# Expert weights w1 and w3 read in 8 KB runs, with token rows transposed by every fourth column

## The chip, the cores and the metric

The kernel runs on one core of a Trainium2 chip, as one program of 34,524 instructions. The metric is the device time of an execution in microseconds; of the kernel before there are three timed runs and one profiled execution. A core has five engines that run side by side: TensorE (PE in the profile, with its weight loads shown apart as PEld), VectorE (DVE), ScalarE (ACT), GpSimd (POOL) and SyncE (SP). SP computes nothing here; it issues most of the transfers between the main memory (DRAM) and the on-chip memory, which 16 DMA engines carry out.

## The reference

One encoder block over 1024 tokens of 1024 channels, in float32. Its first half mixes tokens; its second half, which the change touches, is a mixture of experts:

```
g_logits = xt @ w_rg + b_rg                       # one group of 8
_, g_sel = top_k(g_logits, 1)
e_logits = (xt @ w_re + b_re)[group g_sel]        # 8 experts of that group
top_v, top_i = top_k(e_logits, 2)
weights = softmax(g_logits)[g_sel] * softmax(top_v)
...
hdn = silu(xb @ w1[e]) * (xb @ w3[e])             # w1[e], w3[e]: 1024 x 512
ys  = hdn @ w2[e]                                 # w2[e]: 512 x 1024
out[token] += weight * ys
...
x = layer_norm(ALPHA * x + out)
```

There are 64 experts, each with 6 MB of weights, so the weights of all of them are 403 MB, and each is read once. A matrix product sums over the rows of w1 and w3; in which order it sums does not matter, as long as the tokens' channels are taken in the same order.

## The kernel before, in words

The first half (input projection, convolution, gated linear attention, gates, output projection, first layer norm and router) ends at about 1000 us. It leaves the tokens' rows both in on-chip memory (`x1`) and in a DRAM scratch (`x1_d`).

The expert half works on tiles of 128 rows. Ranked by how many tokens they have, the experts get 128, 64 or 32 rows of a tile, and a fixed string, PATTERN, gives the order of the 29 tiles: an "o" tile is one expert with 128 rows, a "d" tile two with 64, a "q" tile four with 32. For a tile GpSimd clears `xgp` (L1364) and gathers 128 token rows into it with an indirect DMA (`gather`, L1196). `make_xt` (L1204) then transposes `xgp` on TensorE, in 8 blocks of 128 columns, and ScalarE copies the result to `xT` (L1205): 128 partitions, 8 blocks k, 128 tokens. In `make_xt` the operand that the PE loads as weights is the block of `xgp`; what streams past it is the identity matrix.

`job_h` (L1420) multiplies one expert's rows: for k from 0 to 7 it takes block k of `xT` and, of w1 and then of w3, the 512 values that each partition holds for block k. After the activation, `job_t` (L1434) transposes the result, and `job_y` (L1452, L1455) multiplies it with w2. `combine` (L1507) adds finished tiles to the tokens' rows by products with 0/1 matrices, woven in between the steps of later jobs.

The weights come through one queue. `w_pieces` cuts an expert into six pieces of 1 MB: w1, w3 and w2 in two halves each. `load_piece` (L941) issues one piece into one slot of 128 partitions x 8 KB; a half of w1 or w3 is 512 rows of 512 values, a half of w2 is 256 rows of 1024 values. The pieces are issued by SP, in the order in which the tiles need them. `pump_w` issues the next piece only when a slot has been given free, and jobs give slots free as they finish with a piece (`release`). About 16 to 19 slots are in use for weights, some three experts ahead. 382 of the 384 pieces are issued by SP, two by GpSimd.

The lines that fix how rows of w1 and w3 lie on the partitions are the DMA's access pattern, here with r = 512 and f = 512,

```
eng.dma_start(out=t.rearrange("p (k f) -> p k f", f=f),
              in_=m.rearrange("o r f -> (o r) f")[i * r:(i + 1) * r].rearrange("(k p) f -> p k f", p=128))
```

by which partition p holds rows p, 128 + p, 256 + p and 384 + p of the half, four runs of 2 KB, and the blocks that `make_xt` transposes, columns (4h + k) x 128 to (4h + k + 1) x 128, whose column p lands on partition p.

Of the kernel before, what the change touches and what calls it, by code (L numbers as in the profile page):

```python
# [54 lines left out]
assert (1 + N64) % 2 == 0 and N32 % 4 == 0  # L55
OVB = NT * 128
RND = float(3 << 22)


def _order():  # L60
# [22 lines left out]
def tile_block(ctx: ExitStack, tc: tile.TileContext, x, w_in, b_in, conv_w, conv_b, conv_ln_g,  # L83
# [5 lines left out]
    out = out[0]  # L89
# [13 lines left out]
    def slot(dt, name):  # L103
        return SP.tile([128, 2048], dt, tag="slot", name=name, bufs=NS)
# [13 lines left out]
    TE = nc.tensor  # L118
# [13 lines left out]
    ident = CP.tile([128, 128], F32, name="ident")  # L132
# [117 lines left out]
    def load_x(i):  # L250
        t = slot(F32, f"x{i}")
        for c in (slice(0, 512), slice(512, DM)) if i < 2 else (slice(0, DM),):
# [9 lines left out]
                      in_=w_in[:, C_F:C_F + 16].rearrange("(k p) c -> p k c", p=128))  # L262
# [606 lines left out]
    def mmb(shape=(128, 512), name="psb"):  # L869
        return PB.tile(list(shape), F32, tag="mm", name=name, bufs=5)  # L870
# [60 lines left out]
    def load_piece(wt, pc, t=None, eng=nc.sync):  # L931
        nm, src, i, e = pc
        if t is None:
            t = slot(F32, f"{nm}_{i}")
        if isinstance(e, int):
            m = src[e:e + 1]
        else:
            m = src[bass.ds(e(), 1)]
        r = 512 if nm != "w2" else 256
        f = 512 if nm != "w2" else 1024  # L940
        eng.dma_start(out=t.rearrange("p (k f) -> p k f", f=f),  # L941
                          in_=m.rearrange("o r f -> (o r) f")[i * r:(i + 1) * r].rearrange("(k p) f -> p k f", p=128))
        wt.setdefault(nm, []).append(t)

    rank_reg = {}
# [25 lines left out]
    def pump_w(eng=nc.sync):  # L971
        while queue and free[0] > 0 and (queue[0][0][0] == "s" or known):
            key, pc = queue.popleft()
            load_piece(wts_of[key], pc, eng=eng)
            free[0] -= 1
# [128 lines left out]
    xgp = CB.tile([128, DM], F32, name="xgp")  # L1104
# [95 lines left out]
    def make_xt(xT):  # L1200
        for h in range(2):
            ps = mmb((128, 4, 128), "psxT")
            for k in range(4):
                TE.transpose(ps[:, k, :], xgp[:, (4 * h + k) * 128:(4 * h + k + 1) * 128], ident)  # L1204
            A.copy(xT[:, 4 * h:4 * h + 4, :], ps)  # L1205

    static_map(0)
# [42 lines left out]
    V.tensor_scalar(c1[:, 0:16], i128[E64], ov, None, op0=OP.is_lt)  # L1250
    V.tensor_reduce(nb, c1[:, 0:16], axis=AX.X, op=OP.add)
    make_xt(rtm[:, 1024:2048].rearrange("p (k t) -> p k t", k=8))
    gather(tix[:, 1:2])
    prw = smb((128, 512), "psrow")
# [37 lines left out]
    rows = rt1[:, 832:1024].rearrange("p (a e) -> p a e", e=64)  # L1292
# [27 lines left out]
    V.tensor_scalar(hi, s16, -63.5, 1.0 / 128.0, op0=OP.add, op1=OP.mult)  # L1320
    V.tensor_scalar(hi, hi, RND, None, op0=OP.add)
    V.tensor_scalar(hi, hi, RND, None, op0=OP.subtract)
    V.scalar_tensor_tensor(lo, hi, -128.0, s16, op0=OP.mult, op1=OP.add)
# [47 lines left out]
    def turn_rows(s):  # L1371
        s["xT"] = WB.tile([128, 8, 128], F32, name="xTp", bufs=2)
        make_xt(s["xT"])
# [242 lines left out]
    class OnUse(dict):  # L1616
# [5 lines left out]
        def __missing__(self, nm):  # L1622
            for pc in w_pieces(self.e):
                if pc[0] == nm:
                    load_piece(self, pc, self.tiles[pc[2]])
            return self[nm]
# [140 lines left out]
```

## Time and profile before

| | us |
|---|---|
| median of three runs | 2072.95 |
| the three runs | 2072.12 to 2077.11 |
| the profiled execution | 2076.78 |
| its span | 2075.0 |

| engine | busy us | share of the span |
|---|---|---|
| PE | 1952.7 | 94% |
| PEld | 1432.0 | 69% |
| DVE | 1023.6 | 49% |
| ACT | 507.6 | 24% |
| POOL | 124.6 | 6% |

The span runs from the first to the last instruction; the execution's time has a little around it. A busy PE is not a PE at its peak: matmuls overlap, and the profile models their ends. The share of 94% is a mean over two halves that are limited in different ways, so the expert half has to be read by stretches. The DMA share is the mean of the 16 engines; it can pass 1 since an engine can have two packets under way at once. [...]

### The profile page before, as it was taken

How to read it: one execution, taken by the hardware profiler on the slowest of the kernel's cores; microseconds unless marked ns; L12 is line 12 of the kernel's file. 1: busy time of each engine (PE TensorE's matmuls, PEld its weight loads, DVE VectorE, ACT ScalarE, POOL GpSimd, SP SyncE). 2: the span in 40 equal slices, each digit the busy share in tenths (PEclk: the TensorE clock that was granted, in tenths of full speed). 3: DMA queues.
4: the chain of work that ended last, by engine and by line, in shares of the span. 5: the costliest groups of instructions: out<-in, count | busy, mean ns of one | idle time of the engine just before them, and what ended most of it. 6: DMA issues, size and time to landing. Idle time of an engine off the chain costs nothing.

```text
span 2075.0 us, 34524 instructions
## 1 busy us (share of the span) xinstructions
PE 1952.7 (94%) x14631; PEld 1432.0 (69%) x14631; DVE 1023.6 (49%) x1483; ACT 507.6 (24%) x959; POOL 124.6 (6%) x130
## 2 busy tenths in 40 slices
PE   8999999999999999999898997999979997999686
PEld 6898889888888778899645565555655565555453
DVE  4777777878886475566631332223312332223156
ACT  5323342232222343211212121111121121121112
POOL 0000000000000130000100000000000000000000
PEclk9999999999999999999899998999999998999898
DMA  5101210243333536256799999999999999999995
GB/s 168 46 21 44 102 66 21 67 144 138 122 122 142 223 106 204 102 197 240 273 368 394 352 393 394 394 394 393 356 393 393 393 393 394 393 392 393 392 394 210
DMA packets 236749, 525.43 MB, mean 253 GB/s; under 512 B 11730, under 2 KB 53802, under 8 KB 236592
## 3 DMA queue, kind: packets, MB, share of 16 engines
q1 hardware_dynamic: 223808, 482.91, 63.0%
q0 software_dynamic: 12784, 40.28, 5.2%
q8 instruction: 116, 1.90, 0.4%
q14 instruction: 41, 0.34, 0.0%
HBM read 496.33 MB, written 34.08 MB: 256 GB/s over the span
## 4 chain that ended last, share of the span: by engine, by line
PE 37%; DMA 9%; DVE 2%; ACT 1%; issue 1%; SPq 1%; POOLq 0%; ACTq 0%
PE psh L1420 16%; PE pscb L1507 9%; DMA w<-in_w_dram 9%; PE psy L1455 6%; PE psy L1452 2%; PE psxT L1204 1%; PE psacc L1544 1%; PE pshT L1434 1%; DVE x L1512 1%; SPq L941 0%; ACT yv L1465 0%; ACT yhl L1484 0%; DVE yhl L1485 0%; PE psbc L1685 0%; DVE rtm L1337 0%
## 5 line engine op out<-in xcount | busy, mean ns | idle before, releaser
L1420 PE MATMUL psh<-w,xTp 128*32 128x128 f32 (+2 forms) x5792 | 442.0, 326 | 68.0 <-DMA w<-in_w_dram 61.6
L1420 PEld LDWEIGHTS psh<-w,xTp 128*32 128x32 f32 (+2 forms) x5792 | 269.9, 124 | 222.0 <-issue 107.6
L586 DVE SCALAR_TENSOR_TENSOR c<-sg,cw,c 128x994 f32<-128x994 f32 (+14 forms) x240 | 310.0, 1292 | 5.4
L1512 DVE TENSOR_TENSOR x<-x,pscb 128x512 f32<-128x512 f32 x240 | 164.2, 687 | 231.1 <-PE pscb L1507 230.5
L1507 PE MATMUL pscb<-yhl,pt 128*128 128x512 f32 x896 | 268.5, 443 | 8.6 <-DVE pt L1500 6.8
L1507 PEld LDWEIGHTS pscb<-yhl,pt 128*128 128x128 f32 x896 | 162.4, 197 | 93.8 <-issue 33.0
L1455 PE MATMUL psy<-w,hT 128*32 128x256 f32 (+1 forms) x1408 | 150.6, 445 | 0.8 <-ACT hT L1436 0.8
L1427 DVE TENSOR_TENSOR hs<-hs,psh 128x128 f32<-128x128 f32 (+2 forms) x65 | 25.4, 391 | 235.6 <-ACT hs L1426 210.3
L1465 ACT COPY yv<-psy 32x256 f32<-32x256 f32 (+1 forms) x174 | 73.7, 423 | 213.2 <-PE psy L1455 211.3
L1436 ACT COPY hT<-pshT 128x128 f32<-128x128 f32 (+2 forms) x65 | 22.8, 350 | 365.6 <-PE pshT L1434 365.6
L1455 PEld LDWEIGHTS psy<-w,hT 128*32 128x32 f32 (+1 forms) x1408 | 56.6, 118 | 71.8 <-issue 51.7
L1485 DVE SCALAR_TENSOR_TENSOR yhl<-yv,tw,yhl 128x1024 fp32r<-128x1024 f32 x19 | 24.4, 1284 | 160.0 <-ACT yhl L1484 150.9
L1364 POOL MEMSET xgp<- 128x1024 f32 x27 | 25.7, 953 | 828.4 <-PE psxT L1204 828.4
L1452 PE MATMUL psy<-w,hT 128*128 128x512 f32 x144 | 64.0, 597 | 0.0
L1485 DVE SCALAR_TENSOR_TENSOR yhl<-psy,tw,yhl 128x512 fp32r<-128x512 f32 x18 | 13.5, 750 | 88.6 <-ACT yhl L1484 87.6
L1205 ACT COPY xTp<-psxT 128x512 f32<-128x512 f32 x56 | 30.1, 590 | 109.4 <-PE psxT L1204 108.9
L1452 PEld LDWEIGHTS psy<-w,hT 128*128 128x128 f32 x144 | 26.8, 190 | 32.5 <-issue 31.2
L1500 DVE TENSOR_TENSOR pt<-iof,ttok 128x256 fp32r<-128x256 f32 (+1 forms) x120 | 47.8, 400 | 0.0
L1426 ACT ACTIVATE hs<-psh 128x128 f32<-128x128 f32 (+2 forms) x65 | 23.5, 361 | 56.8 <-PE psh L1420 56.3
L1204 PEld LDWEIGHTS psxT<-ident,xgp 128*128 128x128 f32 x232 | 27.4, 143 | 9.1 <-issue 4.1
L1204 PE MATMUL psxT<-ident,xgp 128*128 128x128 f32 x232 | 31.1, 278 | 2.4 <-DVEq L1634 1.6
L502 DVE SCALAR_TENSOR_TENSOR st<-st,dec,pskv 128x256 f32<-128x256 f32 x60 | 28.8, 480 | 7.2 <-PE pskv L218 4.0
(653 smaller groups left out, 3849.1 us busy)
## 6 DMA issues: line engine op xcount, KB each, us to landing
w<-in_w_dram SPq DMA_DIRECT2D x382, 1024.0 KB, 14.0
x<-in_x_dram SPq DMA_DIRECT2D x6, 1024.0 KB, 8.2
o_d<-oT POOLq DMA_DIRECT2D x4, 1024.0 KB, 4.4
conv_d<-c POOLq DMA_DIRECT2D x4, 1024.0 KB, 4.7
or<-o_d SPq DMA_DIRECT2D x4, 1024.0 KB, 4.7
og_d<-or POOLq DMA_DIRECT2D x4, 1024.0 KB, 5.2
gb_d<-gb POOLq DMA_DIRECT2D x4, 1024.0 KB, 7.4
o<-og_d SPq DMA_DIRECT2D x4, 1024.0 KB, 5.8
```

The source lines that it names most:

```text
L502: V.scalar_tensor_tensor(o, prev, gla["dec", p][:, hh, c:c + 1], pk[b][:, a, :], op0=OP.mult, op1=OP.add)
L586: V.scalar_tensor_tensor(c[:, s:], u[:, :SEQ - s], w, c[:, s:], op0=OP.mult, op1=OP.add)
L1204: TE.transpose(ps[:, k, :], xgp[:, (4 * h + k) * 128:(4 * h + k + 1) * 128], ident)
L1205: A.copy(xT[:, 4 * h:4 * h + 4, :], ps)
L1420: TE.matmul(p_[j * cap:(j + 1) * cap, :], s["xT"][:, k, so:so + cap], w_[k // 4][:, (k % 4) * 512 + j * n:(k % 4) * 512 + (j + 1) * n], st ...
L1452: TE.matmul(pys[h], lh, w_[:, h * 512:(h + 1) * 512], start=(f == 0), stop=(f == 3))
L1455: TE.matmul(pys[0][j * cap:(j + 1) * cap, 0:n], lh, w_[:, j * n:(j + 1) * n], start=(f == 0), stop=(f == 3), skip_group_check=True)
L1465: (V.tensor_copy if j % 2 and "same" in s and q["last"] else A.copy)(s["y"][so:so + cap, j * n:(j + 1) * n], pys[0][j * cap:(j + 1) * cap, ...
L1485: V.scalar_tensor_tensor(s["hl"][:, 1024 + c:1024 + c + n], y, s["w"], f32(hi), op0=OP.mult, op1=OP.subtract)
L1500: V.tensor_tensor(pts[tt][:, 0:n, :], iof[:, None, :].to_broadcast([128, n, 128]), tk[:, :, None].to_broadcast([128, n, 128]), op=OP.is_equal)
L1507: TE.matmul(ps, pts[tt][:, a, :], s["hl"][:, i * 1024 + h * 512:i * 1024 + (h + 1) * 512], start=(a + i == 0), stop=(a == n - 1 and i == 1))
L1512: V.tensor_tensor(xa, xa, ps, op=OP.add)
```

## The change

Half a matrix of w1 or w3 (512 rows) is laid on the partitions with four neighbouring rows on each: partition p holds rows 4p to 4p + 3, one run of 8 KB in DRAM. Block k of a partition is then row 4p + k. So that the products still match, `make_xt` transposes, for half h and block k, the columns h x 512 + k, h x 512 + k + 4, and so on: every fourth column of `xgp`, 128 of them. w2 is loaded as before, and so is everything else. The two places use the same lists of pieces and the same tiles; on every engine the instructions and their order are the same, and only the shape of 256 transfers and the step of 232 transposes' reads differ.

```diff
+RUNS = ("w1", "w3")
...
         r = 512 if nm != "w2" else 256
         f = 512 if nm != "w2" else 1024
-        eng.dma_start(out=t.rearrange("p (k f) -> p k f", f=f),
-                          in_=m.rearrange("o r f -> (o r) f")[i * r:(i + 1) * r].rearrange("(k p) f -> p k f", p=128))
+        rows = m.rearrange("o r f -> (o r) f")[i * r:(i + 1) * r]
+        if nm in RUNS:
+
+            eng.dma_start(out=t, in_=rows.rearrange("(p k) f -> p (k f)", p=128))
+        else:
+            eng.dma_start(out=t.rearrange("p (k f) -> p k f", f=f), in_=rows.rearrange("(k p) f -> p k f", p=128))
         wt.setdefault(nm, []).append(t)
...
             for k in range(4):
-                TE.transpose(ps[:, k, :], xgp[:, (4 * h + k) * 128:(4 * h + k + 1) * 128], ident)
+                TE.transpose(ps[:, k, :], xgp[:, h * 512 + k:(h + 1) * 512:4], ident)
             A.copy(xT[:, 4 * h:4 * h + 4, :], ps)
```

## Rows read from the trace of the kernel before

**Rows 1.** Line L941, SP: instructions, duration ns min/median/max, first and last start us.

```profile
L941 SPq DMA_DIRECT2D w<-in_w_dram x382: 367/2198/6328, 921.7 to 2030.6; - x191
```

**Rows 2.** Busy time by stretches, from 1078 us on.

```profile
core 0: us, PE busy (x) PEld busy (x) DVE busy (x) ACT busy (x) POOL busy (x), PEclk, DMA share, GB/s
1078.00:1118.00 40.00, 31.77 (x653) 21.88 (x653) 8.12 (x15) 10.63 (x27) 3.88 (x4) 0.99 1.04 394
1118.00:1166.00 48.00, 46.22 (x189) 25.83 (x189) 15.65 (x26) 5.58 (x11) 1.95 (x2) 0.94 1.02 385
...
1190.00:1305.00 115.00, 97.68 (x1300) 66.26 (x1293) 31.09 (x57) 21.95 (x55) 5.85 (x6) 0.94 1.04 394
1305.00:1418.00 113.00, 111.67 (x580) 62.07 (x581) 29.12 (x48) 20.29 (x37) 7.79 (x8) 0.99 1.04 394
1418.00:1500.00 82.00, 82.00 (x507) 48.71 (x509) 26.71 (x47) 11.39 (x20) 3.90 (x4) 1.00 0.99 369
1500.00:1541.00 41.00, 29.71 (x578) 20.74 (x572) 4.63 (x9) 10.75 (x29) 1.95 (x2) 0.95 1.04 393
1541.00:1640.00 99.00, 99.00 (x484) 57.17 (x484) 30.92 (x53) 14.13 (x26) 7.80 (x8) 0.99 1.04 393
1640.00:1771.00 131.00, 117.87 (x1490) 77.01 (x1487) 33.26 (x60) 26.07 (x61) 5.85 (x6) 0.95 1.04 393
1771.00:1982.00 211.00, 191.37 (x1596) 116.44 (x1599) 53.22 (x92) 38.07 (x77) 10.83 (x12) 0.96 1.04 393
1982.00:2034.00 52.00, 47.80 (x406) 24.19 (x406) 31.86 (x55) 7.58 (x17) 0.00 (x0) 0.93 1.04 392
```

**Rows 3.** The same view in steps of 5 us, around the queue's pauses.

```profile
1165.00:1170.00 5.00, 5.00 (x38) 2.79 (x38) 1.50 (x2) 1.38 (x2) 0.00 (x0) 1.00 0.24 50
1170.00:1175.00 5.00, 5.00 (x44) 3.28 (x42) 0.42 (x1) 1.49 (x4) 0.27 (x1) 1.00 0.98 324
...
1475.00:1480.00 5.00, 5.00 (x27) 2.65 (x28) 1.55 (x3) 1.07 (x2) 1.95 (x2) 1.00 0.58 211
```

**Rows 4.** Who waited for whom: us in total, times, longest us.

```profile
POOL xgp L1364 <- PE psxT L1204: 828.4, 27, 62.8
...
PE psh L1420 <- DMA w<-in_w_dram: 61.6, 28, 5.4
...
SPq L941 <- PE psh L1420: 221.4, 110, 26.9
```

**Rows 5.** The chain that ended last: start us, us, what.

```profile
1935.96 32.66 DMA w<-in_w_dram x2
```

**Rows 6.** Busy time in steps of 2 us, columns as in Rows 2.

```profile
1646.00:1648.00 2.00, 2.00 (x6) 0.82 (x5) 0.00 (x0) 0.00 (x0) 0.00 (x0) 1.00 1.04 406
1648.00:1650.00 2.00, 2.00 (x43) 1.22 (x45) 0.69 (x1) 0.00 (x0) 0.00 (x0) 1.00 1.04 408
...
1654.00:1656.00 2.00, 2.00 (x6) 0.95 (x5) 0.00 (x0) 0.00 (x0) 0.00 (x0) 1.00 1.05 385
1656.00:1658.00 2.00, 2.00 (x6) 0.84 (x5) 0.00 (x0) 0.00 (x0) 0.00 (x0) 1.00 1.05 386
...
1662.00:1664.00 2.00, 2.00 (x23) 1.49 (x13) 0.49 (x1) 0.27 (x1) 0.00 (x0) 1.00 1.04 410
```

**Rows 7.** Line L1204, token transposes: duration ns min/median/max; below, idle time before them.

```profile
L1204 PEld LDWEIGHTS psxT<-ident,xgp x232: 137/141/229, 1013.2 to 1976.7; 128*128 128x128 f32 x116
L1204 PE MATMUL psxT<-ident,xgp x232: 271/273/473, 1013.2 to 1976.8; 128*128 128x128 f32 x116
...
  DMA xgp<-x_d,tix: 1.7, 2
```

**Rows 8.** PE in order of time: start us, us, instructions.

```profile
1763.78 1.03 PE L1204 MATMUL psxT<-ident,xgp 128*128 128x128 f32 x8
```

**Rows 9.** DMA queues of instructions: packets, MB, share of 16 engines.

```profile
q8 instruction: 116, 1.90, 0.4%
q14 instruction: 41, 0.34, 0.0%
```

## The prediction

> **What bounds the kernel now.** I read the page first, then busy time by stretches, then waits and chain, and last the DMA rate in steps of 2 us. Only the second half of the span can change: before 921.7 us no expert weight is issued [rows 1]. From about 1078 to 2034 us the DMA share stands at 1.02 to 1.04 in nearly every stretch and about 393 GB/s is moved [rows 2]: the queue of expert weights never rests, except where it has no free slot, at 1165 to 1170 us (50 GB/s; 324 in the 5 us after it) and at 1475 to 1480 us (211 GB/s) [rows 3]. SP there waits for PE to finish with a weight tile [rows 4].
>
> TensorE is the other side of the same race. In five stretches it is short of weights: 1078 to 1118 (busy 31.77 of 40 us), 1190 to 1305 (97.68 of 115), 1500 to 1541 (29.71 of 41), 1640 to 1771 (117.87 of 131) and 1771 to 1982 (191.37 of 211). The idle time is 8.2 + 17.3 + 11.3 + 13.1 + 19.6 = 69.5 us. Between them it is all but full: 46.22 of 48, 111.67 of 113, 82 of 82, 99 of 99 [rows 2]. The waits say the same: PE waits for the DMA of w 61.6 us in 28 places, none over 5.4 us [rows 4], and the chain of what ended last goes through pieces such as 32.66 us that are transfers of w [rows 5]. So the stage alternates. Where a tile uses one expert, PE is slow and the queue fills the slots; where a tile uses four experts of 32 rows, PE empties them and waits. A faster transfer pays in the second kind only, and no more than about 65 us in all.
>
> **Part 1: longer runs.** An expert is six transfers of 1 MiB: four of w1 and w3, whose runs grow from 2 KB to 8 KB, and two of w2, whose runs stay at 4 KB. The trace of before already shows what a longer run does. In the 2 us windows the rate swings with a period of 16 us: 385 to 386 GB/s at its low, 406 to 410 at its high [rows 6]. 16 us at 393 GB/s are 6.29 MB, one expert; four sixths of it come at the low rate, two sixths at the high one, so the low rate is w1 and w3, and the high one w2. I take 386 and 408. With 16 engines a run of 2048 bytes costs 16 x 2048 / 386 GB/s = 84.9 ns of an engine, one of 4096 bytes 16 x 4096 / 408 = 160.6 ns. The difference, 75.7 ns, is 2048 bytes more; about 9 ns are fixed per run. A run of 8192 bytes, which this trace does not show on this queue, is then an estimate of 160.6 + 2 x 75.7 = 312.0 ns, or 420 GB/s.
>
> For one expert that is 4.194 MB / 386 + 2.097 MB / 408 = 10.87 + 5.14 = 16.01 us before and 9.99 + 5.14 = 15.13 us after: 0.88 us or 5.5% less. Bounds: at the worst the longer run helps no more than w2's runs do (408): 10.28 + 5.14 = 15.42 us, 3.7%. At the best the fixed part vanishes (2048 bytes in 75.7 ns, 433 GB/s): 9.69 + 5.14 = 14.83 us, 7.4%.
>
> Time is saved where PE waits, and only by what the queue gains since it last paused or since PE last had a cushion. That is 40 us (1078 to 1118), 130 us (from the end of the pause, 1175, to 1305), 51 us (1490, shortly after the second pause, to 1541), 131 us (1640 to 1771) and 211 us (1771 to 1982), 563 us in all. Per stretch 5.5% are 2.2, 7.2, 2.8, 7.2 and 11.6 us, each less than PE's idle time in it. The sum is 31.0 us; with 3.7% it is 20.8, with 7.4% it is 41.7.
>
> [...] From 1541 to 1640 PE is full (99.00 of 99 us) and the queue only builds a cushion; with few slots I expect it to pause there instead. If the cushion could grow, 5.5% of 99 us, 5.4 us, would come on top. [...]
>
> SP issues as many DMAs as before, in the same order, with the same waits. Longer runs are also longer turns on an engine: the gathers of token rows (8 runs of 4 KB per engine) take turns with them, and 8 turns of 312 instead of 85 ns could add 1.8 us to a gather. POOL waits 828.4 us in 27 places for the previous transposes before it refills [rows 4], 31 us each, and PE waited only 1.7 us for gathers [rows 7]: the cover is there, the cost nothing. Without that cover it would be 29 x 1.8 = 52 us at the very worst.
>
> **Part 2: every fourth column.** 29 gathered tiles are turned by 8 transposes each, 232 in all; the number stays. What changes is how the weight load reads xgp: 128 columns 16 bytes apart instead of side by side. A load takes 141 ns, a transpose 273 ns [rows 7], and the 8 of a tile pass in 1.03 us [rows 8]: one in about 0.13 us, so the loads set the pace. No load of before reads with such a step, so I bound it: 0 extra, or a load that takes twice as long, 232 x 0.141 = 32.7 us of PE. Of these, 38% fall where PE is full (342 of the 904 us from 1078 to 1982), so 12.4 us are lost; the other 20.3 us disappear into the 38.5 us of waiting that remain. A gain has no ground: the load reads as many elements. I take 0, the nearest rows being the plain loads.
>
> [...]
>
> **Sum.** The profiled execution took 2076.8 us (span 2075.0). 2076.8 - 31.0 = 2045.8. The median of the three runs is 3.8 us lower, 2072.95, so I forecast 2042 us.
>
> **The rivals.**
> A. The 8 KB run travels as pieces of 4 KB, so w1 and w3 come at w2's rate: gain 20.8 us, 2052 us. For: nothing over 4 KB shows on the weight queue. Against: other queues of the core do carry packets of 16 KB (116 packets, 1.90 MB) and of 8 KB (41 packets, 0.34 MB) [rows 9]. [...]
> B. Longer runs work, but the strided weight load takes twice as long: 2042 + 12 = 2054 us. For: the loads set the pace of the transposes. Against: nothing in the trace.
> C. Slower than before: the same mechanism, but four times the load (0.56 us). That is 98 us of PE; 37 us land where PE is full, 61 us in the waiting stretches against 38.5 us of wait, so 22 more: 59 - 31 = 28 us slower, 2101 us. The point from which the strided load outweighs the runs: 232 x extra x 0.38 + (232 x extra x 0.62 - 38.5) = 31, extra 0.30 us, a load of 0.44 us, some three times that of now.
> D. The runs do nothing, since the rate is not set by the run's length but by what is read (w2 against w1 and w3): 2073 us. Against: 2048 and 4096 bytes differ in just the way that a fixed part per run gives, and all three sit in the same memory.
>
> **How the numbers follow.** Forecast 0.55, with 2030 to 2048 as its own range (41.7 us of gain or a little clock at one end; a gain of 25 at the other); A 0.18; B 0.13; D 0.06; C 0.08, its milder forms among them. About 0.3%, 6 us, is what a measurement of this kernel can tell from no change. Faster: the forecast, A and B, 0.86. Same: D, 0.06. Slower: C, 0.08. The range of 8 in 10 takes in A and B and ends where they come together (2052 + 12 = 2064): 2026 to 2064 us.
>
> **What would show it.** The packet count of the weight queue must fall by about 98,000 (256 transfers with 128 instead of 512 runs). In windows of 2 us the swing should turn over: w1 and w3 at about 420 GB/s, above w2 at 408. If all is flat at 408, A is right. The weight load at the token transposes should stay at 141 ns; at 280 it is B, over 440 it is C. PE's wait for w should fall from 61.6 to about 30 us, the stretch 1771 to 1982 shrink most, and the pauses for want of a slot grow. The forecast is wrong if the rate rises and the end does not move: then PE, not the queue, set these stretches.

## The result and the profile after

The changed kernel takes 2039.28 us (median of four runs, 2037.15 to 2043.46) against 2073.27 us before (four runs). The ratio is 0.9835 with a 95% interval of 0.9814 to 0.9856: 34 us faster, where 2042 us had been forecast. The profiled execution, at 2043.46 us the slowest of the four, has a span of 2041.7 us, 33.3 us less than before; what follows compares the two spans.

From the page of the changed kernel: GB/s in 40 equal slices of the span, the packets of all queues, and the queue that carries the weights.

```profile
GB/s 171 47 22 44 104 66 23 54 115 182 119 91 119 242 134 172 125 215 207 232 351 409 381 415 416 416 415 404 321 413 416 389 401 416 415 416 416 415 414 171
DMA packets 138957, 525.43 MB, mean 257 GB/s; under 512 B 11730, under 2 KB 53802, under 8 KB 106032
q1 hardware_dynamic: 126272, 482.91, 60.4%
```

The same 525.43 MB come in far fewer packets, and in the expert half the queue moves 415 to 416 GB/s where it does not rest, against 393 and 394 [rows 2]. It rests more often: the slices at 321, 389 and 401.

The stretches of the changed kernel that answer to [rows 2], with the same columns; the ends are moved to the same places of the program (to about 1 us):

```profile
1079.00:1115.00 36.00, 31.98 (x655) 22.07 (x654) 7.86 (x15) 10.74 (x27) 3.90 (x4) 1.00 1.00 411
1115.00:1160.00 45.00, 43.33 (x189) 24.86 (x189) 15.95 (x27) 5.52 (x12) 1.95 (x2) 1.00 1.01 413
1184.00:1292.00 108.00, 98.39 (x1308) 67.70 (x1297) 30.49 (x55) 21.97 (x55) 5.85 (x6) 0.94 1.02 415
...
1404.00:1485.00 81.00, 81.00 (x474) 47.89 (x476) 26.67 (x46) 10.51 (x20) 3.90 (x4) 1.00 0.90 347
1485.00:1524.50 39.50, 29.03 (x608) 20.92 (x600) 4.63 (x9) 11.63 (x29) 1.95 (x2) 1.00 1.02 415
1524.50:1624.00 99.50, 99.47 (x484) 58.16 (x486) 30.89 (x53) 14.13 (x26) 7.81 (x8) 0.98 1.00 405
1624.00:1745.00 121.00, 115.20 (x1491) 75.52 (x1485) 33.15 (x60) 26.06 (x61) 5.85 (x6) 0.97 1.01 408
1745.00:1947.00 202.00, 189.68 (x1592) 116.21 (x1592) 53.30 (x93) 38.08 (x77) 10.83 (x12) 0.97 1.02 416
```

PE's idle time (length less PE busy) in the five stretches that were short of weights is now 4.0, 9.6, 10.5, 5.8 and 12.3 us, 42.2 in all against 69.5: 27.3 us less waiting (by stretch 4.2, 7.7, 0.8, 7.3 and 7.3 us less). In the two full stretches from 1404 to 1485 and from 1524.5 to 1624 us PE still works without a gap, and in the first of them the queue rests longer than before (347 GB/s against 369). In the full stretch from 1115 to 1160 us PE passes 189 instructions in 43.33 us, where it took 46.22 before. The waits agree, in the view of who waited for whom of the changed kernel:

```profile
PE psh L1425 <- DMA w<-in_w_dram: 34.7, 20, 5.3
```

That is 34.7 us in 20 places instead of 61.6 in 28 [rows 4], 26.9 us less. The other 6 us are not waiting. The page's PE line says so, of before and then of after:

```profile
PE 1952.7 (94%) x14631; PEld 1432.0 (69%) x14631; DVE 1023.6 (49%) x1483; ACT 507.6 (24%) x959; POOL 124.6 (6%) x130
```

```profile
PE 1947.3 (95%) x14630; PEld 1432.8 (70%) x14631; DVE 1024.0 (50%) x1483; ACT 507.6 (25%) x959; POOL 124.2 (6%) x130
```

PE is busy 5.4 us less with the same instructions, while its granted clock (PEclk in the views, the share of its full speed that PE was given) rose from 0.973 to 0.979 over the span. 27.3 + 5.4 = 32.7 of the 33.3 us. Two later profiles of the changed kernel (the runs that serve as a measure below) have spans of 2039.1 and 2036.6 us, with PE busy 1943.3 and 1941.6 us at a clock of 0.979 and 0.981. In the span before, PE is idle for 122.3 us, in the three of the changed kernel for 94.4, 95.8 and 95.0. So the waiting that went is much the same in all three, 26.5 to 27.9 us; the busy time that went varies, 5.4, 9.4 and 11.1 us.

Where along the program the time came out can be read at products that start the moment their weights land. The timeline of PE, of before and then of after: start, length, instructions, in brackets the idle time before them and what ended it.

```profile
1118.11 6.54 PE L1420 MATMUL psh<-w,xTp 128*128 128x512 f32 x8 [4.67 <-DMA w<-in_w_dram]
...
1540.80 4.45 PE L1420 MATMUL psh<-w,xTp 128*64 128x256 f32 x26 [5.19 <-DMA w<-in_w_dram]
...
1770.80 1.10 PE L1420 MATMUL psh<-w,xTp 128*128 128x512 f32 x2 [2.38 <-DMA w<-in_w_dram]
...
1981.94 0.43 PE L1420 MATMUL psh<-w,xTp 128*32 128x128 f32 x8 [1.22 <-DMA w<-in_w_dram]
```

```profile
1114.97 3.67 PE L1425 MATMUL psh<-w,xTp 128*128 128x512 f32 x8 [0.26 <-DMA w<-in_w_dram]
...
1524.53 1.98 PE L1425 MATMUL psh<-w,xTp 128*64 128x256 f32 x8 [4.75 <-DMA w<-in_w_dram]
...
1745.27 1.10 PE L1425 MATMUL psh<-w,xTp 128*128 128x512 f32 x2 [1.19 <-DMA w<-in_w_dram]
...
1947.15 0.43 PE L1425 MATMUL psh<-w,xTp 128*32 128x128 f32 x8 [1.54 <-DMA w<-in_w_dram]
```

The four are 3.1, 16.3, 25.5 and 34.8 us earlier, so the parts between them gave 3.1, 13.1, 9.3 and 9.3 us; behind the last one, where PE no longer waits for weights, 1.5 us are lost again.

The first of the four shows the clock too. The same 8 products take 6.54 us before and 3.67 us after, 2.87 us less. Before, PE had waited 4.67 us for weights and then ran at a granted clock of 0.50; after, it had waited 0.26 us and ran at 1.00. Busy time behind that wait, before and then after, columns as in [rows 2]:

```profile
1118.10:1121.00 2.90, 2.89 (x4) 1.35 (x5) 0.00 (x0) 0.00 (x0) 0.00 (x0) 0.50 1.05 386
```

```profile
1115.00:1118.00 3.00, 3.00 (x7) 1.37 (x8) 0.29 (x1) 0.02 (x1) 0.00 (x0) 1.00 1.01 415
```

In both later profiles of the changed kernel the 8 products take 3.67 us as well.

### The profile page after: what moved, and what is told of

It reads as the page before. It is cut to its first block, busy times and chain, and to the rows that moved or that the text cites. A ratio compares the mean times of both kernels' runs of the same rounds, so it can differ in the third digit from the quotient of the medians.

```text
span 2041.7 us, 34523 instructions
## 1 busy us (share of the span) xinstructions
PE 1947.3 (95%) x14630; PEld 1432.8 (70%) x14631; DVE 1024.0 (50%) x1483; ACT 507.6 (25%) x959; POOL 124.2 (6%) x130
## 2 busy tenths in 40 slices
DMA packets 138957, 525.43 MB, mean 257 GB/s; under 512 B 11730, under 2 KB 53802, under 8 KB 106032
## 5 line engine op out<-in xcount | busy, mean ns | idle before, releaser
L1425 PE MATMUL psh<-w,xTp 128*32 128x128 f32 (+2 forms) x5792 | 436.1, 324 | 40.6 <-DMA w<-in_w_dram 34.7
L1512 PE MATMUL pscb<-yhl,pt 128*128 128x512 f32 x896 | 264.4, 436 | 8.1 <-DVE pt L1505 6.8
L1209 PEld LDWEIGHTS psxT<-ident,xgp 128*128 128x128 f32 x232 | 32.2, 207 | 8.0 <-issue 3.7
```

The source lines that it names most:

```text
L1209: TE.transpose(ps[:, k, :], xgp[:, h * 512 + k:(h + 1) * 512:4], ident)
L1425: TE.matmul(p_[j * cap:(j + 1) * cap, :], s["xT"][:, k, so:so + cap], w_[k // 4][:, (k % 4) * 512 + j * n:(k % 4) * 512 + (j + 1) * n], st ...
L1512: TE.matmul(ps, pts[tt][:, a, :], s["hl"][:, i * 1024 + h * 512:i * 1024 + (h + 1) * 512], start=(a + i == 0), stop=(a == n - 1 and i == 1))
```

## The experiments

The theory: a run has a fixed cost of about 9 ns (an estimate from 386 and 408 GB/s), so a longer run carries its bytes faster; the time comes out only where PE waits for weights; and the strided weight load costs PE something on the path (at first put at 6 us). The rivals were that the gain has another cause, that every long run counts alike, and that the strided load is hidden or weighs in full. All experiments were timed against the kernel before in the same rounds, whose median there was 2074.5 to 2075.2 us. The changed kernel itself, run twice more as a measure, took 2038.49 us and 2038.50 us (ratios 0.9822, 0.9809 to 0.9836, and 0.9826, 0.981 to 0.9842).

**The runs alone.** The transposes read neighbouring columns again. They leave out the matching of channels to rows of w1 and w3; the amount of work is the same.

```diff
-                TE.transpose(ps[:, k, :], xgp[:, h * 512 + k:(h + 1) * 512:4], ident)
+                TE.transpose(ps[:, k, :], xgp[:, (4 * h + k) * 128:(4 * h + k + 1) * 128], ident)
```

> w1 and w3 in 8 KB runs, but token rows transposed by neighbouring columns as before (so channels and weight rows are matched wrongly; only the time is of interest). Theory 1, the strided weight load costs PE 232 x 68 ns = 15.8 us and 38% of that is on the path: 6 us faster than the changed kernel, about 2033 us, weight load back to 141 ns, waits of PE for w above the 34.7 us of the changed kernel. Rival, the strided load is hidden under the waits for weights: about 2039 us. Other rival, all of it is on the path: about 2023 us.

Measured: 2038.86 us, ratio 0.9824 (0.981 to 0.9838), the same as with the strided transposes. PE's wait for w is 36.5 us, no more than in the three profiles of the changed kernel (34.7, 37.2 and 35.7).

**The stride alone.** The kernel before with the changed line of the transposes only; channels and rows are again not matched.

```diff
-                TE.transpose(ps[:, k, :], xgp[:, (4 * h + k) * 128:(4 * h + k + 1) * 128], ident)
+                TE.transpose(ps[:, k, :], xgp[:, h * 512 + k:(h + 1) * 512:4], ident)
```

> Before, with w1 and w3 in 2 KB runs, but token rows transposed by every fourth column (matched wrongly again). Theory 1, 38% of 15.8 us on the path: about 2079 us, weight load 209 ns, PE's wait for w down from 61.6 to about 52 us. Rival, hidden: 2073 us. Other rival, all on the path: 2089 us.

Measured: 2075.57 us, ratio 1.0003 (0.9993 to 1.0013), and PE's wait for w 57.0 us, between the 61.6 of before and the 52 of the theory. Both runs say that the stride costs nothing that can be told from noise, at most 2.7 us by this interval; the 6 us were wrong. The instructions of the line in this kernel, and one tile's transposes in its timeline, show why:

```profile
L1204 PEld LDWEIGHTS psxT<-ident,xgp x232: 195/209/226, 1014.0 to 1977.6; 128*128 128x128 f32 x116
L1204 PE MATMUL psxT<-ident,xgp x232: 270/283/487, 1014.0 to 1977.7; 128*128 128x128 f32 x116
```

```profile
1174.22 1.12 PE L1204 MATMUL psxT<-ident,xgp 128*128 128x128 f32 x8
```

The load did grow, from 141 to 209 ns, but the 8 transposes of a tile only from 1.03 [rows 8] to 1.12 us. The recorded time of a load is not what it costs, since loads run side by side: 232 at 209 ns would be 48.5 us, but the time in which any of them is under way is 32.20 us (27.43 before). The line's busy time in all, before and then in this kernel: length, PE busy, PEld busy, granted clock, DMA share, GB/s.

```profile
1000.00:2075.00 1075.00, 31.07 (x232) 27.43 (x232) 0.95 0.99 374
```

```profile
1000.00:2075.00 1075.00, 33.34 (x232) 32.20 (x232) 0.95 1.00 375
```

So 68 ns more of load are some 10 ns more per transpose, 2.3 us of PE over 29 tiles and not 15.8.

**Runs of 4 KB.** w1 and w3 as pairs of neighbouring rows, the transposes with a step of two.

```diff
-            eng.dma_start(out=t, in_=rows.rearrange("(p k) f -> p (k f)", p=128))
+            eng.dma_start(out=t.rearrange("p (a g) -> p a g", a=2), in_=rows.rearrange("(a p k) f -> p a (k f)", a=2, k=2))
...
-                TE.transpose(ps[:, k, :], xgp[:, h * 512 + k:(h + 1) * 512:4], ident)
+                TE.transpose(ps[:, k, :], xgp[:, h * 512 + k // 2 * 256 + k % 2:h * 512 + (k // 2 + 1) * 256:2], ident)
```

> w1 and w3 in two runs of 4 KB per partition (pairs of neighbouring rows), token rows transposed by every second column to match. Theory 1, a fixed cost of about 9 ns per run sets the rate: w1 and w3 at w2's 408 GB/s, the 2 us windows flat at 406 to 410, gain of about 21 us of transfer plus the 3 us by which the changed kernel beat that sum, less what a step of 8 bytes costs the weight load (between 0 and the 68 ns seen for 16 bytes): 2049 to 2055 us. Rival, the gain comes from neighbouring rows being on one partition at all, or from w1 and w3 being slow for another reason than the run: rate at 386 or at 416 GB/s, 2073 or 2040 us.

Measured: 2049.28 us, ratio 0.988 (0.9863 to 0.9896). Three of its 2 us windows, columns as in [rows 6] (the three before them read 406, 412 and 406):

```profile
1706.00:1708.00 2.00, 2.00 (x6) 0.73 (x4) 0.00 (x0) 0.54 (x1) 0.00 (x0) 1.00 1.03 410
1708.00:1710.00 2.00, 2.00 (x68) 1.79 (x71) 1.71 (x3) 1.11 (x3) 0.00 (x0) 1.00 1.03 410
1710.00:1712.00 2.00, 2.00 (x52) 1.67 (x42) 0.66 (x3) 0.00 (x0) 0.00 (x0) 1.00 1.03 410
```

The swing between w1, w3 and w2 is gone and all travel at w2's rate: it is the length of the run that sets the rate, not the matrix, and not neighbouring rows as such. The run also answers a rival that was not named, that the changed kernel is faster because more transfers are under way at once. Here a piece lands 18.0 us after its issue instead of 14.0, about seven pieces under way instead of five, and yet 4 KB runs travel at 408 to 409 GB/s in the slices of its page, as w2 did before. SP's issue takes 2129 ns in the median here, nearly as long as before (2198), so the issue does not set the rate either.

**Sorting the columns at the store.** One ScalarE copy per tile sorts the columns before the rows are stored for the gathers, so that the transposes read without a step.

```diff
+        xq = WB.tile([128, DM], F32, name="xq", bufs=1)
+        for h in range(n):
+            c = slice(h * DM // n, (h + 1) * DM // n)
+            A.copy(xq[:, c].rearrange("p (h k q) -> p h k q", k=4, q=128), xv[:, c].rearrange("p (h q k) -> p h k q", k=4, q=128))
-        G.dma_start(out=x1_d[tt * 128:(tt + 1) * 128, :], in_=xv)
+        G.dma_start(out=x1_d[tt * 128:(tt + 1) * 128, :], in_=xq)
```

> 8 KB runs as in the changed kernel; the columns are sorted when the token rows are stored for the gathers (one ScalarE copy of 128 x 1024 per tile into an extra buffer, 8 copies), so the transposes read neighbouring columns again. Theory 1: weight load 141 ns, gain of the run alone (as in the experiment with the runs only, about 2033 us) less 1 to 2 us for the last copy before the first gather: about 2035 us. Rival, the strided load was hidden: 2040 to 2041 us, no better than the changed kernel.

Measured: 2047.18 us, ratio 0.9871 (0.9855 to 0.9888): 8 us slower than the changed kernel, which neither side expected. The kernel has one such buffer (`bufs=1`), and ScalarE, behind whose copies the router's copies are queued, waited for its stores; from the waits of this kernel between 900 and 1030 us:

```profile
ACT xq L1002 <- DMA x_d<-xq: 26.9, 5, 7.5
...
PE pslg L1023 <- ACT x1T L1017: 5.5, 1, 5.5
```

The first token transposes begin at 1023.1 instead of 1014.0 us. There was nothing to win, and the way around it cost 9 us at once.

**Short runs where PE is full, and short runs where it waits.** In two kernels 12 experts each go back to 2 KB runs (48 of the 256 transfers) and their tiles to transposes without a step. The diff is of the first; the second has ranks 20 to 27 and 52 to 55.

```diff
+SHORT = {("r", i) for i in (3, 4, 5, 6, 10, 11, 12, 13, 14, 15, 18, 19)}
...
-        if nm in RUNS:
+        if nm in RUNS and not short:
...
-            load_piece(wts_of[key], pc, eng=eng)
+            load_piece(wts_of[key], pc, eng=eng, short=key in SHORT)
```

> The changed kernel, but 12 experts (48 of the 256 transfers of w1 and w3) go back to 2 KB runs and to transposes of neighbouring columns; they are those of the d and o tiles with ranks 3 to 6, 10 to 15, 18 and 19, whose weights travel while PE is full and does not wait. Theory, time is saved only where PE waits for weights: no loss, 2039 to 2041 us; the queue pauses less. Rival, every long run counts alike: 48 of 256 of the 34 us are lost, 6.4 us, 2046 us.

> The same with 12 other experts, ranks 20 to 27 and 52 to 55, whose weights travel in the last stretch, at the end of which PE waits. Theory: all of the 12 x 0.88 us = 10.6 us are lost, about 2050 us, PE's wait for w up by about 10 us from 34.7. Rival, every long run counts alike: 2046 us.

Measured: 2040.77 us, ratio 0.9837 (0.982 to 0.9854), and 2050.69 us, ratio 0.9883 (0.9865 to 0.99). Against the changed kernel in the same rounds (2038.49 us) the same number of short runs costs 2.3 us, within the intervals, in one place, and 12.2 us in the other; 10.6 had been worked out. The short runs are where they were meant to be: in the first kernel slices between 1323 and 1425 us read 394 GB/s, in the second the last stretch moves 394 instead of 416. In the first the queue also rests less (366 GB/s in the slice around 1450 us, against 317 in the run of the changed kernel with it). PE's wait for weights, of the first and of the second:

```profile
PE psh L1426 <- DMA w<-in_w_dram: 35.0, 20, 4.4
```

```profile
PE psh L1426 <- DMA w<-in_w_dram: 42.2, 23, 5.4
```

The second wait grew by 7.5 us over 34.7 (by 5.0 over the 37.2 of the changed kernel run with it), less than the 10 expected; what the rest of the 12.2 us is was not followed up. So a long run is worth much only where a wait follows that the queue cannot have made up by then.

**w2 in 8 KB runs too.** The even and odd hidden columns go into separate blocks, first by reading w1 and w3 with a step of two as the streamed operand everywhere.

```diff
+                    wv = w_[k // 4][:, (k % 4) * 512:(k % 4 + 1) * 512].rearrange("p (i x b) -> p i b x", i=2, b=2)
+                    wv = wv if T == 1 else wv[:, j] if T == 2 else wv[:, j // 2, j % 2]
```

> w2 in 8 KB runs too (two neighbouring rows per partition); to match, the products with w1 and w3 read every second column of a weight row as the streamed operand, which puts the even and the odd hidden columns into separate blocks. Theory of a fixed cost per run: the six transfers of an expert take 6.291 MB / 420 = 14.98 us instead of 15.13, 1.0% of some 560 us, 5 us faster than the changed kernel: 2034 us. Rival: a step of 8 bytes slows the streamed operand as it slowed the weight load (141 to 209 ns): if the products of L1425, 436 us busy, grow by even a tenth, PE is the bound and the time is over 2060 us.

Measured: 2044.14 us, ratio 0.9842 (0.9827 to 0.9858), between the two expectations. It is 5.7 us slower than the changed kernel run with it; the intervals overlap, but four of its five executions lie above all five of the other. The rate rises to 420 GB/s as worked out (the slices of its page), and PE's streams grow by less than a tenth, but by enough. The products with w1 and w3 of one-expert tiles, of the changed kernel run with it and of this one:

```profile
L1425 PE MATMUL psh<-w,xTp 128*128 128x512 f32 x288 | 135.9, 597 | 5.8 <-DMA w<-in_w_dram 5.8
```

```profile
L1423 PE MATMUL psh<-w,xTp 128*128 128x512 f32 x288 | 142.0, 617 | 2.0 <-DMA w<-in_w_dram 2.0
```

PE was busy 1960.2 us against 1943.3 in that run of the changed kernel, 16.9 us more, for the 5 us of transfer that had been worked out. The last version keeps the step where it is cheap, in the transposes before the product with w2:

```diff
+            hc = slice(0, 128) if nbk == 1 else slice(c // 2 * 256 + c % 2, (c // 2 + 1) * 256, 2)
-            TE.transpose(ps[:, c, :], q["hs"][:, c * 128:(c + 1) * 128], ident)
+            TE.transpose(ps[:, c, :], q["hs"][:, hc], ident)
...
+                    if T == 4:
+                        wv = slice((k % 4) * 512 + j // 2 * 256 + j % 2, (k % 4) * 512 + (j // 2 + 1) * 256, 2)
```

> All weights in 8 KB runs as in the experiment with w2, but the step of two columns is moved to where it is cheap: for tiles of one and two experts to the transposes before the product with w2 (strided weight load, 209 instead of 141 ns, hidden beside the previous transpose), for tiles of four experts it stays in the streamed operand of the products with w1 and w3 (their 138 us grow by about 4 us, in the tiles that wait for weights). Theory: the 5 us of transfer come through and at most 1 or 2 us are lost to PE: 2034 to 2036 us. Rival: transfers no longer bound enough of the stage, no gain: 2039 us.

Measured: 2037.36 us, ratio 0.982 (0.9804 to 0.9835), beside 2038.50 us and 0.9826 for the changed kernel: no difference that can be told. PE's wait for w is 28.7 us there, and the queue at 420 GB/s, but PE is busy 1950.6 us against 1941.6. What the transfer still gave, PE took, as far as one profile of each can say.

## Why the prediction was right, step by step

1. *The price of a run.* Worked out as 312 ns for 8192 bytes, 420 GB/s, and 6.29 MB in 15.13 us for an expert, which is 416 GB/s for w1, w3 and w2 together. Measured: 415 to 416 in the long stretches without a pause (411 and 413 in the two before 1160 us), and 420 where every run has 8 KB. Rival A (pieces of 4 KB) would have been flat at 408 to 410, as the run with 4 KB was; D fell with the same run.
2. *Where it pays.* That only the stretches with waits count was borne out by the two kernels with short runs, 2.3 against 12.2 us. The sizes by stretch were less good. Up to the product at 1118 us 2.2 were forecast and 3.1 came, then 7.2 + 2.8 = 10.0 and 13.1, then 7.2 and 9.3, then 11.6 and 9.3. Of the 13.1 us, 2.87 are the 8 products at 1118 us, which ran at a granted clock of 1.00 instead of 0.50. Of the third part, waiting fell by 7.3 us, as forecast, and PE's busy time by 2.7 (117.87 to 115.20, at a clock of 0.97 instead of 0.95), so that excess too goes with the clock; of the cushion that was priced at nothing (5.4 us from 1541 to 1640) nothing is to be seen. The last part fell short. Its sum took the same bytes to be moved between the two ends, but 202 us at 416 GB/s are 84.0 MB, against 82.9 in 211 us at 393: one piece more, some 2.5 us. Why one more had to be moved stays open.
3. *The waits.* 38.5 us of waiting were to remain and 42.2 did. The transfer gave 27.3 us of waiting and not 31.0.
4. *The clock.* The forecast counts nothing for it, and "a little clock" stands only at one end of its range. No run shows that term; what the runs showed in its place is that 5.4 us of PE's busy time went, at a granted clock of 0.979 instead of 0.973, and 9.4 and 11.1 us in the two later profiles. This is the term that was mis-sized, and it fills the gap left by the one before it: that the total came within 3 us of the forecast is in part luck, two misses that cancel. In [rows 2] the granted clock is 0.94 to 0.96 in four of the five waiting stretches, where a faster PE only waits longer, but it is also 0.94 in the full stretch from 1118 us: the low clock, 0.50, stood at its head, and 2.87 us came out there at once. There the clock is shown; for the rest of the busy time it is argued. All 14 executions of the changed kernel had a clock of 0.979 to 0.982, the 35 of the kernel before that were timed beside the experiments 0.970 to 0.976, but no run changes the clock alone.
5. *The strided transposes.* 0 was right by luck, its ground was wrong. The load did not stay at 141 ns, it grew by half, to 209, within the bounds; at the prediction's own price that would have been 15.8 us of PE, 6 of them on the path. The step that failed is "the loads set the pace": it took the recorded time of a load for what the load costs. Loads overlap, and 68 ns more each came to 10 ns per transpose of PE's time, of which no run shows any on the path. The price per load in B and C was too high for the same reason. What makes the 68 ns no run shows; with a step of two columns, 8 bytes, the load also takes 209 ns, in the kernel with runs of 4 KB:

```profile
L1209 PEld LDWEIGHTS psxT<-ident,xgp x232: 194/209/226, 1011.1 to 1950.5; 128*128 128x128 f32 x116
```

6. *The signs asked for.* Packets fell by 97,792 over all queues (236,749 before), about 98,000 had been said. The swing did not turn over to be seen: nine 2 us windows of the changed kernel, from 1700 to 1718 us, scatter between 393 and 432 GB/s, so the rate of w1 and w3 rests on the stretches, not on windows. PE's wait fell to 34.7 us and not to about 30. The pauses grew, as said. The gathers, for which up to 1.8 us more each had been estimated, landed 8.0 us after their issue in the median instead of 7.1; PE waited 1.6 us for them, where it had waited 1.7 [rows 7]. The last stretch did not shrink most: it lost 9 us (211 to 202), the one before it 10 (131 to 121).

## What to carry to other kernels

Two run lengths in one trace were enough here to work out the cost of a third (420 GB/s from 386 and 408, and 420 where every run has 8 KB): split the rate by transfer, solve for a fixed part and a part per byte, and check the sum against the period. Then count the faster transfer only where the consumer waits, from the queue's last pause on (the same number of short runs cost 2.3 us in one place and 12.2 in the other), and look for what the consumer pays for the new layout: a step in an operand whose loads overlap cost nothing that could be measured here (ratio 1.0003), a step in the streamed operand added three times as much PE work as the transfer that it was reckoned to save (16.9 us for 5).

## What the runs showed of the hardware that was not expected

SP's issue of a weight transfer took 2198 ns in the median before [rows 1] and takes 345 ns in the changed kernel:

```profile
L945 SPq DMA_DIRECT2D w<-in_w_dram x254: 327/345/1762, 922.5 to 1989.3; - x127
```

Transfers are queued deeper instead. From issue to landing a piece takes 20.0 us instead of 14.0 in the pages' lists of DMA issues, and SP now waits mostly for earlier transfers of w rather than for PE, as its queue's waits in the changed kernel show:

```profile
SPq L945 <- DMA w<-in_w_dram: 299.2, 167, 3.3
SPq L947 <- DMA w<-in_w_dram: 164.7, 84, 2.7
...
SPq L945 <- PE psh L1425: 85.8, 60, 8.2
```

At about 2.5 us a piece (1.049 MB at 416 GB/s) 20.0 us are, as an estimate, eight pieces under way, where 14.0 us at 2.7 us were five. The deeper queue gave nothing by itself that shows: with 4 KB runs and about seven under way the rate was 408 to 409 GB/s, that of w2's 4 KB runs with five.
